# A two-block transformer kernel: the modulation as sums along rows of the transposed weight, and head gains loaded once per partition

## The chip, the core and the metric

The program runs on one core of one Trainium2 chip. The metric is the device time of one execution in microseconds (us); times of before are a median of three runs.

## What is computed

The reference is two transformer blocks over 256 tokens of width 1024, all in fp32: the first with three attention branches, a memory attention and a gated feed-forward layer, the second with a forgetting attention, a retention and an MLP. The second block is modulated: six vectors of 1024 come from one condition vector c, and the outputs of its heads are normalized with a gain of their own.

```
c_act = silu(c)                                        # c: 1 x 1024
mod = einsum('bd,de->be', c_act, w_ada) + b_ada        # w_ada: 1024 x 6144
shift_m, scale_m, gate_m, shift_f, scale_f, gate_f = split(mod, 6)
h = rms(x) * (1 + scale_m) + shift_m
...
fq = rms(fq) * q_norm_gain;  fk = rms(fk) * k_norm_gain            # gains of 64, the same for 8 heads
fox = (rms(fox) * fox_out_gain) * sigmoid(f_og)
ret = (rms(ret) * ret_out_gain) * silu(r_gate)
x = x + gate_m * (concat(fox, ret) @ w_out)
h = rms(x) * (1 + scale_f) + shift_f
x = x + gate_f * (square(relu(h @ w_mlp_in)) @ w_mlp_out)
```

## The kernel before

Tokens stand in two tiles of 128 partitions. Every weight comes as tiles `raw` of 128 x 1024 fp32 (0.5 MB), which ScalarE rounds to `wh` and VectorE (DVE) turns into the rest `wl` (`cols`); each product is then three matmuls (`mm3`). A norm ends in `transpose_split`: TensorE transposes the normed tile `xn` and ScalarE and DVE write it as `aT`, which the next matmuls read. The last products of a stage are done for token tile 0 first and then, behind it, for tile 1 (`out_steps`), so that the norm of tile 0 runs beside the matmuls of tile 1.

The program is written as generators that record operations (`Plan.add`); nothing of it is issued in the order of the code. `Plan.run` goes through a model of time with a price for every operation (`cost`), gives each engine the operation that is due first, and gives tiles their slots in pools of fixed size (`SLOTS`: 12 tiles of 1 KB a partition, 14 of 2 KB, 37 of 4 KB and small ones). What comes out is one fixed order for each engine; each engine works through its own in order, and SyncE issues all transfers in one order. `TUNING` shifts due times by windows of matmuls. All instructions carry line 629, where they are issued, so groups are told apart by the names of their tiles.

The modulation is cut into 12 parts of 512 columns (`modulation`, `mod_part`, started by `next_part` in the merge of the first block, in its feed-forward layer and in the MLP). A part clears `acc` on GpSimd (POOL), loads the bias into its first row, loads `w_ada` with 8 of its rows to a partition, and adds them up on DVE with c as a scalar of each partition, 8 sums of 128 x 512. Then POOL sums over the 128 partitions, and the row goes to DRAM (`mod_rows`). `mod(i)` reads it back as a row broadcast to all partitions, `modrow`:

```
for j0 in range(0, 8, 2):
    nc.sync.dma_start(r, self.mod_w[:, j0:j0 + 2, c0:c0 + 512])
    for j in range(2):
        nc.vector.scalar_tensor_tensor(acc, r[:, j, :], self.mod_c[:, j0 + j:j0 + j + 1], acc, ALU.mult, ALU.add)
nc.gpsimd.partition_all_reduce(acc, acc, channels=P, reduce_op=bass_isa.ReduceOp.add)
```

POOL also does the powers of all norms (`rstd`, `row_rstd`: `s<-s,mhalf`). In `block2_mix`, `rep_row` loads the two gains of 64 repeated 8 times into `qkg`, and the output gains into `og`, which line 1986 scales by 0.5 on DVE: the gates are computed as 1 + tanh of half the argument, which is twice the sigmoid.

Of the kernel before, what the change touches and what calls it, by code (L numbers as in the profile page):

```python
# [16 lines left out]
ALU = mybir.AluOpType  # L17
# [10 lines left out]
EPS = 1e-6  # L28
# [245 lines left out]
class Plan:  # L274
# [146 lines left out]
    @staticmethod  # L421
    def cost(o, views):
        if not views:
            return 1.29
        n = max(math.prod(v.shape[1:]) for v in views)
        psum = any(v.root.kind == "ps" for v in views)
        if o.eng == "pe":
            if o.name == "transpose":
                return 0.11
            n, dt = math.prod(o.args[0].shape[1:]), o.args[1].dtype  # L430
            one = max(0.213, n / 600) if dt == F32 else max(0.104 if dt == F32R else 0.054, n / 2400)
            return one * (0.6 if dt == F32 and o.args[0].shape[0] in (32, 64) else 1.0) + 0.003
        if o.eng == "act":
            return (0.051 if psum else 0.094) + n / 1200 + 0.093 * (isinstance(o.kw.get("scale"), View)
                                                                    + isinstance(o.kw.get("bias"), View) + ("accum_out" in o.kw))
        if o.eng == "dve":
            if o.name == "reciprocal":
                return 0.07 + 0.0062 * n
            fast = not psum and o.name in ("tensor_copy", "tensor_scalar")
            small = o.name in ("tensor_scalar", "scalar_tensor_tensor") and len(views) > (2 if fast else 3)  # L440
            return 0.068 + n / (1920 if fast else 960) + 0.06 * small
        if o.eng == "pool":
            if o.name == "partition_all_reduce":
                return 3.57
# [187 lines left out]
class Net:  # L632
# [133 lines left out]
        yield  # L766


    def rstd(self, ssq, n, width):
        nc = self.nc  # L770
        ms = self.small(n)
        nc.vector.tensor_scalar(ms, ssq, 1.0 / width, EPS, ALU.mult, ALU.add)
        r = self.small(n)
        nc.gpsimd.tensor_tensor(r, ms, self.mhalf[:, :n], ALU.pow)
        return r
# [904 lines left out]


    def modulation(self):
        nc, a = self.nc, self.a
        self.mod_w = a["w_ada_2"].rearrange("(p j) n -> p j n", p=P)
        self.mod_rows = self.tile("dram", DM, nm="mod_rows")[0:6]
        c, s = (self.fixed(8, f"mod_{n}") for n in "cs")
        nc.sync.dma_start(c, a["c_2"].rearrange("a (p j) -> (a p) j", p=P))
        nc.vector.tensor_scalar(s, c, -80.0, None, ALU.max)
        nc.scalar.activation(s, s, AF.Exp, scale=-1.0)
        nc.vector.tensor_scalar(s, s, 1.0, None, ALU.add)  # L1690
        nc.vector.reciprocal(s, s)
        nc.vector.tensor_tensor(s, s, c, ALU.mult)
        self.mod_c = s

    def mod_part(self, q):

        nc = self.nc
        c0 = q * 512
        acc = self.k(2, [P, 512], nm="mod")
        nc.gpsimd.memset(acc, 0.0)  # L1700
        nc.sync.dma_start(acc[0:1, :], self.a["b_ada_2"][:, c0:c0 + 512])
        for j0 in range(0, 8, 2):
            raw = self.k(4, [P, 1024], nm="raw")
            r = raw.rearrange("p (k n) -> p k n", k=2)
            nc.sync.dma_start(r, self.mod_w[:, j0:j0 + 2, c0:c0 + 512])
            yield
            for j in range(2):
                nc.vector.scalar_tensor_tensor(acc, r[:, j, :], self.mod_c[:, j0 + j:j0 + j + 1], acc, ALU.mult, ALU.add)
        yield
        nc.gpsimd.partition_all_reduce(acc, acc, channels=P, reduce_op=bass_isa.ReduceOp.add)  # L1710
        if q // 2 in (1, 4):
            yield
            nc.vector.tensor_scalar(acc, acc, 1.0, None, ALU.add)
        yield
        nc.sync.dma_start(self.mod_rows[q // 2:q // 2 + 1, c0 % DM:c0 % DM + 512], acc[0:1, :])

    def next_part(self):
        if not self.mod_parts:
# [41 lines left out]
    def block2_mix(self, x, u, done):  # L1760
        nc, a, flow = self.nc, self.a, self.flow
# [14 lines left out]
        raw = self.k(4, [P, DM], nm="onehot")  # L1776
# [1 line left out]
        nc.sync.dma_start(raw[:40], a["const_b"][:40, slice(*AT_B["onehot"])])  # L1778
        nc.scalar.activation(onehot.rearrange("p a b -> p (a b)"), raw, AF.Copy)

        def rep_row(src, n, rep, off, tl):
            nc.sync.dma_start(tl[:, off:off + n * rep].rearrange("p (a b) -> p a b", a=rep),
                              bass.AP(tensor=src.tensor, offset=src.offset, ap=[[0, P], [0, rep], [1, n]]))

        qkg = self.k(4, [P, DM], nm="qkg")
        rep_row(a["q_norm_gain_2"], 64, 8, 0, qkg)
        rep_row(a["k_norm_gain_2"], 64, 8, 512, qkg)
        og = self.k(4, [P, DM], nm="og")
        rep_row(a["fox_out_gain_2"], 512, 1, 0, og)
        rep_row(a["ret_out_gain_2"], 512, 1, 512, og)  # L1790
        bf = self.small(8)
        src = a["b_forget_2"]
        nc.sync.dma_start(bf, bass.AP(tensor=src.tensor, offset=src.offset, ap=[[0, P], [1, 8]]))
# [3 lines left out]
        spl = [None, None]  # L1797
        v, rv = ([h[:, 0, :] for h in self.two(nm, (1, 512))] for nm in ("fv", "rv"))

        def head_rstd(src, nh, d):  # L1800
            sq = self.k(2, [P, nh, d], nm="sq")
            nc.scalar.activation(sq, src, AF.Square)
            yield
            ss = self.small(nh)
            nc.vector.tensor_reduce(ss, sq, AX, ALU.add)
            r = self.rstd(ss, nh, d)
            yield
            return r
# [347 lines left out]
```

## Time and profile before

| | |
|---|---|
| time, median of 3 runs | 787.75 us (786.53 to 788.32) |
| the profiled execution: time, span | 789.33 us, 787.5 us |
| TensorE (PE) busy | 750.9 us, 95% |
| DVE busy | 601.9 us, 76% |
| ACT (ScalarE), POOL busy | 393.2 us, 95.2 us |
| mean granted TensorE clock | 0.979 |
| HBM read | 159.68 MB, mean 204 GB/s |

The page's share of busy time tells which engine is full; the time that can be saved lies where PE is not. PEld is the loading of weights into TensorE beside PE. "issue" in a bracket is time in which an engine waited for nothing that the profile shows.

### The profile page before, as it was taken

How to read it: one execution, taken by the hardware profiler on the slowest of the kernel's cores; microseconds unless marked ns; L12 is line 12 of the kernel's file. 1: busy time of each engine (PE TensorE's matmuls, PEld its weight loads, DVE VectorE, ACT ScalarE, POOL GpSimd, SP SyncE). 2: the span in 40 equal slices, each digit the busy share in tenths (PEclk: the TensorE clock that was granted, in tenths of full speed). 3: DMA queues.
4: the chain of work that ended last, by engine and by line, in shares of the span. 5: the costliest groups of instructions: out<-in, count | busy, mean ns of one | idle time of the engine just before them, and what ended most of it. 6: DMA issues, size and time to landing. Idle time of an engine off the chain costs nothing.

```text
span 787.5 us, 13291 instructions
## 1 busy us (share of the span) xinstructions
PE 750.9 (95%) x5195; PEld 684.6 (87%) x5195; DVE 601.9 (76%) x937; ACT 393.2 (50%) x650; POOL 95.2 (12%) x74
## 2 busy tenths in 40 slices
PE   6999999979998999999999389999999999999998
PEld 3989899979897999999998268898887999999996
DVE  4999999979799996978463388889759897755522
ACT  5685684336378434344252165564646644554510
POOL 0111002222000220222200022011101022000000
PEclk9999999989999999999999769999999999999999
DMA  9819566937584597999783538445436885654501
GB/s 313 288 61 271 165 227 218 349 152 264 180 277 150 181 330 265 293 297 312 253 263 80 187 90 198 104 142 172 167 113 249 286 288 212 220 193 166 178 1 54
DMA packets 93811, 161.63 MB, mean 205 GB/s; under 512 B 8019, under 2 KB 44019, under 8 KB 93748
## 3 DMA queue, kind: packets, MB, share of 16 engines
q1 hardware_dynamic: 93748, 160.78, 61.7%
q8 instruction: 41, 0.67, 0.3%
q14 instruction: 22, 0.18, 0.1%
HBM read 159.68 MB, written 1.07 MB: 204 GB/s over the span
## 4 chain that ended last, share of the span: by engine, by line
PE 68%; DVE 6%; DMA 4%; issue 2%; POOL 1%; ACT 0%; SPq 0%; POOLq 0%; DVEq 0%
PE ps L629 68%; DMA og<-in_fox_out_gain_dram 3%; DVE wl L629 1%; DVE x L629 1%; DMA raw<-in_w_in_dram 1%; DVE xn L629 1%; DVE mod L629 1%; DVE s L629 0%; POOL s L629 0%; DVE mk L629 0%; DVE mg L629 0%; DVE mgt L629 0%; DVE prob L629 0%; DVE mq L629 0%; DVE gt L629 0%
## 5 line engine op out<-in xcount | busy, mean ns | idle before, releaser
L629 DVE TENSOR_TENSOR wl<-raw,wh 128x1024 fp32r<-128x1024 f32 (+4 forms) x237 | 292.3, 1259 | 42.9 <-ACT wh L629 27.7
L629 PE MATMUL ps<-aT,wh 128*128 128x256 f32 x1664 | 308.3, 285 | 0.0
L629 ACT ACTIVATE wh<-raw 128x1024 fp32r<-128x1024 f32 (+5 forms) x237 | 240.9, 1042 | 129.4 <-DMA raw<-in_w_ffn_in_dram 30.0
L629 PEld LDWEIGHTS ps<-aT,wh 128*128 128x128 f32 x1664 | 259.2, 189 | 0.7 <-issue 0.4
L629 PE MATMUL ps<-aT,wl 128*128 128x256 f32 x832 | 236.5, 284 | 0.0
L629 PE MATMUL ps<-wh,aT 128*128 128x512 f32 (+5 forms) x672 | 184.6, 360 | 1.2 <-ACT aT L629 0.7
L629 PEld LDWEIGHTS ps<-aT,wl 128*128 128x128 f32 x832 | 157.3, 189 | 0.8 <-issue 0.8
L629 PE MATMUL ps<-wh,hT 128*128 128x512 f32 (+1 forms) x540 | 140.4, 349 | 0.0
L629 PEld LDWEIGHTS ps<-wh,aT 128*128 128x128 f32 x672 | 119.7, 192 | 18.7 <-ACT aT L629 1.3
L629 PE MATMUL ps<-wl,aT 128*128 128x512 f32 (+5 forms) x336 | 118.2, 356 | 0.0
L629 PEld LDWEIGHTS ps<-wh,hT 128*128 128x128 f32 x540 | 94.0, 188 | 14.2
L629 PE MATMUL ps<-wl,hT 128*128 128x512 f32 (+1 forms) x270 | 94.2, 349 | 0.0
L629 DVE SCALAR_TENSOR_TENSOR mod<-raw,mod_s,mod 128x512 f32<-128x512 f32 x96 | 75.3, 786 | 2.3 <-DMA raw<-in_w_ada_dram 1.0
L629 POOL PARTITION_ALL_REDUCE mod<-mod x12 | 49.8, 4148 | 220.2 <-DVE mod L629 212.0
L629 PEld LDWEIGHTS ps<-wl,aT 128*128 128x128 f32 x336 | 64.0, 191 | 8.0 <-DVE wl L629 0.3
L629 PEld LDWEIGHTS ps<-wl,hT 128*128 128x128 f32 x270 | 50.8, 188 | 7.1
L629 POOL TENSOR_TENSOR s<-s,mhalf 128x1 f32<-128x1 f32 (+3 forms) x22 | 24.3, 1108 | 211.6 <-DVE s L629 171.9
L629 PE MATMUL ps<-ident,xn 128*128 128x128 f32 x96 | 23.6, 354 | 26.7 <-DVE xn L629 26.6
L629 PEld LDWEIGHTS ps<-ident,xn 128*128 128x128 f32 x96 | 14.5, 175 | 33.4 <-issue 20.0
L629 ACT ACTIVATE junk<-x 128x512 f32<-128x512 f32 (+1 forms) x29 | 16.0, 554 | 51.2 <-DVE x L629 49.5
L629 DVE TENSOR_TENSOR relu<-relu 128x512 f32<-128x512 f32 x16 | 10.9, 692 | 23.8 <-ACT relu L629 23.7
L629 ACT ACTIVATE aT<-ps 128x256 fp32r<-128x256 f32 (+1 forms) x41 | 17.9, 459 | 21.7 <-PE ps L629 21.4
(280 smaller groups left out, 656.4 us busy)
## 6 DMA issues: line engine op xcount, KB each, us to landing
raw<-in_w_in_dram SPq DMA_DIRECT2D x62, 512.0 KB
raw<-in_w_ada_dram SPq DMA_DIRECT2D x48, 512.0 KB
raw<-in_w_ffn_in_dram SPq DMA_DIRECT2D x44, 512.0 KB
raw<-in_w_mlp_in_dram SPq DMA_DIRECT2D x32, 512.0 KB
raw<-in_w_mlp_out_dram SPq DMA_DIRECT2D x32, 512.0 KB
raw<-in_w_ffn_out_dram SPq DMA_DIRECT2D x22, 512.0 KB
raw<-in_w_out_dram SPq DMA_DIRECT2D x16, 512.0 KB
raw<-in_w_up_dram SPq DMA_DIRECT2D x6, 512.0 KB
```

What stands on the lines that cost most here:

```text
L629: getattr(get[o.eng], name)(*map(real, args), **{k: real(v) for k, v in kw.items()})
```

## The change

The weight of the modulation is given to the kernel transposed (6144 rows of 1024): a layout of the input, made on the host. Of vector i, partition p then holds the 8 outputs p*8 to p*8+7, one row of 1024 each. c is stored to DRAM and read back as a row broadcast to all partitions; each row is multiplied with it on DVE and summed along the row by the same instruction (`accum_out`), 48 sums of 128 x 1024 in all. The results, 8 columns for each vector, get the bias (and 1.0 for the two scales) in one small operation and go to `mod_rows` as 128 pieces of 32 B; the bias is loaded once, as 128 x 6 x 8. The parts run where they ran, two for each vector.

The head gains are loaded once for each partition and broadcast over the 8 heads in the operand of the product. The output gains are not scaled: the 0.5 goes into the power, by multiplying mean square and epsilon with 4 (`part=0.5`). The planner's price of partition_all_reduce is dropped. The planner then orders the whole program anew.

```diff
-    def rstd(self, ssq, n, width):
+    def rstd(self, ssq, n, width, part=1.0):
...
-        nc.vector.tensor_scalar(ms, ssq, 1.0 / width, EPS, ALU.mult, ALU.add)
+        nc.vector.tensor_scalar(ms, ssq, part ** -2 / width, EPS * part ** -2, ALU.mult, ALU.add)
...
     def modulation(self):
...
-        self.mod_w = a["w_ada_2"].rearrange("(p j) n -> p j n", p=P)
-        self.mod_rows = self.tile("dram", DM, nm="mod_rows")[0:6]
-        c, s = (self.fixed(8, f"mod_{n}") for n in "cs")
+        self.mod_w = a["w_ada_2"].rearrange("(i p j) k -> i p j k", i=6, p=P)
+        self.mod_rows = self.tile("dram", DM, nm="mod_rows")[0:7]
+        self.mod_b, self.mod_s = self.fixed(48, "mod_b"), self.fixed(48, "mod_s")
+        nc.sync.dma_start(self.mod_b.rearrange("p (i j) -> p i j", i=6),
+                          a["b_ada_2"].rearrange("a (i p j) -> (a p) i j", i=6, p=P))
+        c, s = (self.small(8, f"mod_{n}") for n in "cs")
...
-        self.mod_c = s
+        nc.sync.dma_start(self.mod_rows[6:7, :].rearrange("a (p j) -> (a p) j", p=P), s)
+        self.mod_c = self.k(4, [P, DM], nm="mod_c")
+        nc.sync.dma_start(self.mod_c, self.mod_rows[6:7, :].to_broadcast([P, DM]))
...
     def mod_part(self, q):
...
+        i = q // 2
+        for j in range(q % 2 * 4, q % 2 * 4 + 4):
+            raw = self.k(4, [P, DM], nm="raw")
+            nc.sync.dma_start(raw, self.mod_w[i, :, j, :])
+            yield
+            nc.vector.scalar_tensor_tensor(raw, raw, 1.0, self.mod_c, ALU.mult, ALU.mult,
+                                           accum_out=self.mod_s[:, i * 8 + j:i * 8 + j + 1])
         yield
-        nc.gpsimd.partition_all_reduce(acc, acc, channels=P, reduce_op=bass_isa.ReduceOp.add)
...
+        if q % 2:
+            s, b = (m[:, i * 8:i * 8 + 8] for m in (self.mod_s, self.mod_b))
+            nc.vector.scalar_tensor_tensor(s, s, 1.0 if i in (1, 4) else 0.0, b, ALU.add, ALU.add)
+            yield
+            nc.sync.dma_start(self.mod_rows[i:i + 1, :].rearrange("a (p j) -> (a p) j", p=P), s)
...
-        qkg = self.k(4, [P, DM], nm="qkg")
-        rep_row(a["q_norm_gain_2"], 64, 8, 0, qkg)
-        rep_row(a["k_norm_gain_2"], 64, 8, 512, qkg)
+        qkg = self.k(1, [P, 2 * 64], nm="qkg")
+        rows(a["q_norm_gain_2"], 64, 0, qkg)
+        rows(a["k_norm_gain_2"], 64, 64, qkg)
...
-                gain = qkg[:, which * 512:(which + 1) * 512].rearrange("p (a b) -> p a b", b=64)
+                gain = qkg[:, None, which * 64:(which + 1) * 64].to_broadcast([P, 8, 64])
...
-            r = yield from head_rstd(mv, nh, d)
+            r = yield from head_rstd(mv, nh, d, 0.5)
...
-        nc.vector.tensor_scalar(og, og, 0.5, None, ALU.mult)
...
+    return {"w_ada_2": np.ascontiguousarray(given["w_ada_2"][0].T)}
```

How the order moves, at three places. The numbers behind the names are those of single tiles.

First, DVE where the second block's norm begins (`block2_norm`; x_68 is the stream, ps the sums of the feed-forward layer). Before:

```order
L629 TENSOR_TENSOR hT_5166<-silu_5091,hT_5166 128x512
L629 TENSOR_TENSOR wl_5176<-raw_5057,wh_5155 128x1024
L629 TENSOR_SCALAR og_5138<-og_5138 128x1024
L629 TENSOR_TENSOR x_68<-ps_3535,x_68 128x512
L629 TENSOR_TENSOR x_68<-ps_3542,x_68 128x512
L629 TENSOR_TENSOR x_68<-x_68,gain_4852 128x512 x2
```

Now:

```order
L627 TENSOR_TENSOR hT_5088<-silu_5021,hT_5088 128x512
L627 TENSOR_TENSOR wl_5098<-raw_4984,wh_5077 128x1024
L627 TENSOR_TENSOR x_68<-ps_3502,x_68 128x512
L627 TENSOR_TENSOR x_68<-ps_3509,x_68 128x512
L627 TENSOR_TENSOR x_68<-x_68,gain_4781 128x512 x2
```

The scaling of og between the last weight and the residual sums is gone; the rest stands as it stood.

Second, POOL around the norm of the memory (the two powers of a 128x1 tile, `s<-s,mhalf`). The ISA rows with names are the reductions over partitions; those without stand wherever POOL goes from them to its other operations and back. Before:

```order
L629 MEMSET mod_1152 128x512
L629 MEMSET mod_1173 128x512
L629 MEMSET mod_1182 128x512
L629 MEMSET mod_1629 128x512
L629 ISA
L629 ISA mod_1152<-mod_1152 128x512
L629 ISA mod_1173<-mod_1173 128x512
L629 ISA mod_1182<-mod_1182 128x512
L629 ISA
L629 TENSOR_TENSOR s_2181<-s_2181,mhalf_70 128x1
L629 TENSOR_TENSOR s_2184<-s_2184,mhalf_70 128x1
L629 ISA
```

Now:

```order
L627 COPY cn_845<-qcn_993 128x64
L627 COPY cn_845<-qcn_1000 128x64
L627 TENSOR_TENSOR s_2197<-s_2197,mhalf_70 128x1
L627 TENSOR_TENSOR s_2200<-s_2200,mhalf_70 128x1
L627 TENSOR_TENSOR s_2625<-s_2625,mhalf_70 128x1
```

Nothing stands between the copies of the sparse attention and the powers, and the next norm's power follows at once.

Third, DVE between the memory attention (`prob` its weights, moT its output) and the residual sums of x. Before:

```order
L629 TENSOR_SCALAR prob_3007<-prob_3007,s_3047 128x256 x4
L629 COPY mv_3070<-ps_2921 128x256
L629 TENSOR_TENSOR wl_3074<-raw_2758,wh_2880 128x1024
L629 TENSOR_TENSOR wl_3092<-raw_2768,wh_2893 128x1024
L629 TENSOR_TENSOR moT_3105<-ps_3081,moT_3105 128x2x128
L629 TENSOR_TENSOR wl_3110<-raw_2822,wh_2913 128x1024
L629 TENSOR_TENSOR moT_3105<-ps_3096,moT_3105 128x2x128
L629 TENSOR_TENSOR wl_3125<-raw_2942,wh_3043 128x1024
L629 TENSOR_TENSOR x_68<-ps_3114,x_68 128x512
```

Now:

```order
L627 TENSOR_SCALAR prob_2953<-prob_2953,s_3007 128x256 x2
L627 TENSOR_TENSOR wl_3054<-raw_2796,wh_2908 128x1024
L627 TENSOR_TENSOR wl_3060<-raw_2942,wh_3011 128x1024
L627 TENSOR_TENSOR wl_3074<-raw_2948,wh_3022 128x1024
L627 TENSOR_TENSOR wl_3087<-raw_2958,wh_3042 128x1024
L627 TENSOR_TENSOR wl_3091<-raw_2967,wh_3058 128x1024
L627 TENSOR_TENSOR moT_3093<-ps_3078,moT_3093 128x2x128
L627 SCALAR_TENSOR_TENSOR raw_3062,mod_s_1657<-raw_3062,mod_c_1470 128x1024
L627 TENSOR_TENSOR moT_3093<-ps_3045,moT_3093 128x2x128
L627 SCALAR_TENSOR_TENSOR raw_3068,mod_s_1657<-raw_3068,mod_c_1470 128x1024
L627 TENSOR_TENSOR x_68<-ps_3097,x_68 128x512
```

Five splits of a weight and two sums of the modulation stand there in place of four splits.

## Rows read from the trace of the kernel before

**Rows 1.** The page, its parts 1 and 2: busy time, share of the span and number of instructions of each engine; and, in 40 equal slices of the span (19.7 us each), the busy share of DVE and the granted TensorE clock, in tenths.

```profile
PE 750.9 (95%) x5195; PEld 684.6 (87%) x5195; DVE 601.9 (76%) x937; ACT 393.2 (50%) x650; POOL 95.2 (12%) x74
...
DVE  4999999979799996978463388889759897755522
...
PEclk9999999989999999999999769999999999999999
```

**Rows 2.** [...]

```profile
160.00:180.00 20.00, 15.68 (x110) 14.66 (x109) 14.12 (x21) 8.99 (x12) 6.05 (x4) 0.83 0.38 142
...
200.00:220.00 20.00, 20.00 (x130) 18.06 (x129) 15.54 (x26) 8.02 (x18) 2.55 (x3) 1.00 0.64 203
...
220.00:240.00 20.00, 19.70 (x176) 18.47 (x174) 19.14 (x40) 15.88 (x37) 0.00 (x0) 1.00 0.83 276
...
240.00:260.00 20.00, 17.23 (x111) 15.71 (x111) 17.80 (x34) 14.29 (x29) 1.74 (x3) 0.91 0.36 119
...
440.00:460.00 20.00, 4.80 (x12) 2.48 (x12) 13.30 (x29) 9.48 (x26) 4.12 (x5) 0.61 0.55 188
```

**Rows 3.** PE in order of time around us 440: start, duration, operation, and in brackets the idle time before it and what ended it.

```profile
430.33 0.39 PE L629 MATMUL ps<-wl,hT 128*128 128x512 f32 x1
...
438.84 0.28 PE L629 MATMUL ps<-wl,hT 128*128 128x256 f32 x1
...
452.69 1.27 PE L629 MATMUL ps<-ident,xn 128*128 128x128 f32 x4 [13.58 <-DVE xn L629]
```

**Rows 4.** DVE in order of time, same stretch, same columns.

```profile
446.11 0.69 DVE L629 TENSOR_SCALAR og<-og 128x1024 f32<-128x1024 f32 x1 [20.06 <-DMA og<-in_ret_out_gain_dram]
...
446.71 1.28 DVE L629 TENSOR_TENSOR x<-ps,x 128x512 f32<-128x512 f32 x2
...
456.16 0.98 DVE L629 TENSOR_SCALAR x<-x,s 128x1024 f32<-128x1024 f32 x1
```

**Rows 5.** The DMA queue of SyncE in order of time: when a transfer is issued and how long the issue takes.

```profile
419.45 0.38 SPq L629 DMA_DIRECT2D qkg<-in_q_norm_gain_dram  x1
...
420.50 5.02 SPq L629 DMA_DIRECT2D og<-in_fox_out_gain_dram  x1
```

**Rows 6.** Stretches of 4 us around us 440, columns as in rows 2.

```profile
420.00:424.00 4.00, 4.00 (x29) 3.68 (x28) 1.51 (x2) 1.30 (x2) 0.00 (x0) 1.00 0.10 31
...
452.00:456.00 4.00, 1.68 (x6) 1.13 (x7) 3.94 (x8) 2.87 (x8) 1.44 (x3) 0.50 0.18 66
...
456.00:460.00 4.00, 3.12 (x8) 1.35 (x6) 3.96 (x11) 3.74 (x11) 1.97 (x3) 0.50 0.52 119
...
460.00:464.00 4.00, 4.00 (x14) 3.25 (x14) 3.56 (x10) 2.61 (x6) 0.00 (x0) 0.50 0.25 79
...
464.00:468.00 4.00, 4.00 (x17) 3.19 (x16) 3.39 (x3) 2.79 (x4) 0.00 (x0) 0.89 0.45 94
```

**Rows 7.** PE in order of time around us 170.

```profile
172.05 0.47 PE L629 MATMUL ps<-ident,xn 128*128 128x128 f32 x1 [3.64 <-DVE xn L629]
```

**Rows 8.** Stretches of 4 us behind it, columns as in rows 2.

```profile
172.00:176.00 4.00, 3.27 (x12) 2.46 (x13) 4.00 (x7) 0.00 (x0) 0.00 (x0) 0.50 0.02 5
176.00:180.00 4.00, 4.00 (x28) 4.00 (x27) 3.96 (x7) 2.83 (x5) 1.64 (x1) 0.73 0.77 271
```

**Rows 9.** POOL in order of time, us 120 to 185.

```profile
159.16 4.14 POOL L629 PARTITION_ALL_REDUCE mod<-mod  x1 [17.30 <-DVE mod L629]
170.62 1.12 POOL L629 TENSOR_TENSOR s<-s,mhalf 128x1 f32<-128x1 f32 x2 [7.32 <-issue]
```

**Rows 10.** DVE in order of time, us 148 to 182.

```profile
160.37 3.27 DVE L629 SCALAR_TENSOR_TENSOR mod<-raw,mod_s,mod 128x512 f32<-128x512 f32 x2
...
171.24 2.74 DVE L629 SCALAR_TENSOR_TENSOR xn<-mx,s,gain 128x512 f32<-128x512 f32 x4 [5.81 <-POOL s L629]
```

**Rows 11.** PE at the norm ahead of the last MLP, in order of time.

```profile
602.19 1.23 PE L629 MATMUL ps<-ident,xn 128*128 128x128 f32 x6 [0.99 <-DVE xn L629]
```

**Rows 12.** Stretches behind the norms at us 250 and 600, columns as in rows 2.

```profile
250.00:252.00 2.00, 2.00 (x11) 2.00 (x11) 2.00 (x6) 1.01 (x3) 0.00 (x0) 0.50 0.00 0
...
252.00:254.00 2.00, 2.00 (x14) 2.00 (x14) 1.49 (x5) 1.98 (x4) 0.00 (x0) 0.68 0.00 0
...
600.00:610.00 10.00, 8.90 (x42) 6.50 (x42) 9.56 (x19) 8.39 (x15) 0.82 (x2) 1.00 0.97 368
```

**Rows 13.** Instructions of the tile mod (sums of the modulation): number, min/median/max ns, first and last start, forms.

```profile
L629 DVE SCALAR_TENSOR_TENSOR mod<-raw,mod_s,mod x96: 732/747/2732, 112.0 to 654.9; 128x512 f32<-128x512 f32 x96
```

**Rows 14.** The same for the tile wl (low parts of the weights).

```profile
L629 DVE TENSOR_TENSOR wl<-raw,wh x237: 622/1219/3266, 11.9 to 748.6; 128x1024 fp32r<-128x1024 f32 x111, 128x452 fp32r<-128x452 f32 x2, 128x768 fp32r<-128x768 f32 x2, 128x904 fp32r<-128x904 f32 x1
```

**Rows 15.** Groups of instructions, shapes apart: number, busy us, mean ns, idle time before them.

```profile
L629 DVE TENSOR_TENSOR aT<-ps,aT 128x512 fp32r<-128x512 f32 x15 | 9.9, 685 | 0.6 <-ACT aT L629 0.6
...
L629 ACT ACTIVATION_READ_ACCUMULATOR junk<-x 128x1 f32 x29 | 5.4, 186 | 0.0
```

**Rows 16.** Stretch of 1 us in the first loads, columns as in rows 2.

```profile
20.00:21.00 1.00, 1.00 (x7) 0.92 (x6) 1.00 (x2) 1.00 (x3) 0.00 (x0) 1.00 1.07 393
```

**Rows 17.** ACT in order of time, us 0 to 70: the first split of a weight that was issued after the loads of the modulation.

```profile
31.40 1.06 ACT L629 ACTIVATE wh<-raw 128x1024 fp32r<-128x1024 f32 x1
```

**Rows 18.** The DMA queue of SyncE in order of time, us 66 to 160, columns as in rows 5.

```profile
99.59 3.15 SPq L629 DMA_DIRECT2D raw<-in_w_up_dram  x2
...
110.50 1.71 SPq L629 DMA_DIRECT2D raw<-in_w_ada_dram  x2
```

More of the change, by code (lines that the diff above doesn't have):

```diff
@@ L442, in cost @@
         if o.eng == "pool":
-            if o.name == "partition_all_reduce":
-                return 3.57
             if o.name == "memset":
@@ L1692, in modulation @@
         nc.vector.tensor_tensor(s, s, c, ALU.mult)
-        self.mod_c = s
+        nc.sync.dma_start(self.mod_rows[6:7, :].rearrange("a (p j) -> (a p) j", p=P), s)
+        self.mod_c = self.k(4, [P, DM], nm="mod_c")
+        nc.sync.dma_start(self.mod_c, self.mod_rows[6:7, :].to_broadcast([P, DM]))
     def mod_part(self, q):
         nc = self.nc
[L1698 to L1705, printed above, removed]
+        i = q // 2
+        for j in range(q % 2 * 4, q % 2 * 4 + 4):
+            raw = self.k(4, [P, DM], nm="raw")
+            nc.sync.dma_start(raw, self.mod_w[i, :, j, :])
             yield
-            for j in range(2):
-                nc.vector.scalar_tensor_tensor(acc, r[:, j, :], self.mod_c[:, j0 + j:j0 + j + 1], acc, ALU.mult, ALU.add)
+            nc.vector.scalar_tensor_tensor(raw, raw, 1.0, self.mod_c, ALU.mult, ALU.mult,
+                                           accum_out=self.mod_s[:, i * 8 + j:i * 8 + j + 1])
         yield
-        nc.gpsimd.partition_all_reduce(acc, acc, channels=P, reduce_op=bass_isa.ReduceOp.add)
-        if q // 2 in (1, 4):
+        if q % 2:
+            s, b = (m[:, i * 8:i * 8 + 8] for m in (self.mod_s, self.mod_b))
+            nc.vector.scalar_tensor_tensor(s, s, 1.0 if i in (1, 4) else 0.0, b, ALU.add, ALU.add)
             yield
-            nc.vector.tensor_scalar(acc, acc, 1.0, None, ALU.add)
-        yield
-        nc.sync.dma_start(self.mod_rows[q // 2:q // 2 + 1, c0 % DM:c0 % DM + 512], acc[0:1, :])
+            nc.sync.dma_start(self.mod_rows[i:i + 1, :].rearrange("a (p j) -> (a p) j", p=P), s)
     def next_part(self):
@@ L1779, in block2_mix, with rows @@
         nc.scalar.activation(onehot.rearrange("p a b -> p (a b)"), raw, AF.Copy)
-        def rep_row(src, n, rep, off, tl):
-            nc.sync.dma_start(tl[:, off:off + n * rep].rearrange("p (a b) -> p a b", a=rep),
-                              bass.AP(tensor=src.tensor, offset=src.offset, ap=[[0, P], [0, rep], [1, n]]))
-        qkg = self.k(4, [P, DM], nm="qkg")
-        rep_row(a["q_norm_gain_2"], 64, 8, 0, qkg)
-        rep_row(a["k_norm_gain_2"], 64, 8, 512, qkg)
+        def rows(src, n, off, tl):
+            nc.sync.dma_start(tl[:, off:off + n], bass.AP(tensor=src.tensor, offset=src.offset, ap=[[0, P], [1, n]]))
+        qkg = self.k(1, [P, 2 * 64], nm="qkg")
+        rows(a["q_norm_gain_2"], 64, 0, qkg)
+        rows(a["k_norm_gain_2"], 64, 64, qkg)
         og = self.k(4, [P, DM], nm="og")
-        rep_row(a["fox_out_gain_2"], 512, 1, 0, og)
-        rep_row(a["ret_out_gain_2"], 512, 1, 512, og)
+        rows(a["fox_out_gain_2"], 512, 0, og)
+        rows(a["ret_out_gain_2"], 512, 512, og)
         bf = self.small(8)
@@ L1798, in block2_mix, with head_rstd @@
         v, rv = ([h[:, 0, :] for h in self.two(nm, (1, 512))] for nm in ("fv", "rv"))
-        def head_rstd(src, nh, d):
+        def head_rstd(src, nh, d, part=1.0):
             sq = self.k(2, [P, nh, d], nm="sq")
@@ L1805, in head_rstd @@
             nc.vector.tensor_reduce(ss, sq, AX, ALU.add)
-            r = self.rstd(ss, nh, d)
+            r = self.rstd(ss, nh, d, part)
             yield
@@ L2131, in views @@
     for k, ap in aps.items():
-        if k in ("b_ada_2", "c_2", "norm_final", "const_a", "const_b"):
+        if k in ("b_ada_2", "c_2", "w_ada_2", "norm_final", "const_a", "const_b"):
             out[k] = ap
@@ L2136, in views, with EXTRA @@
     return out
+def EXTRA(given):
+    return {"w_ada_2": np.ascontiguousarray(given["w_ada_2"][0].T)}
 def kernel(**inputs):
@@ L2146 @@
     given["const_a"], given["const_b"] = CONST_A, CONST_B
+    given.update(EXTRA(given))
     for name, arr in given.items():
```

## The prediction

> **What bounds the kernel now.** I read the page first: TensorE is busy for 750.9 of 787.5 us, DVE for 601.9 [rows 1]. So time can only come out of the 36.6 us in which PE idles, and out of the slices in which its clock is not granted. The clock line has one dip, where the second block's normalization begins [rows 1]. The table of stretches then shows where PE idles: 15.20 us in us 440 to 460, 4.32 in 160 to 180, 2.77 in 240 to 260 [rows 2]; most of the rest is the first loads and the last store. I call these places A (440), B (170) and C (250). Each is a norm that every following matmul needs.
>
> At **A** the list of PE shows the last matmul at 438.84 and the first transposition at 452.69, 13.58 us later, released by DVE [rows 3]. The list of DVE says why: its queue stood 20.06 us at the scaling of og by 0.5, which waited for og's load; the residual sum x<-ps, the head of the norm, is the very next instruction [rows 4]. And og came late because the gains qkg were issued ahead of it [rows 5], each row copied 8 times to each of 128 partitions, 2048 pieces of 256 B: behind their issue the queue moved 31 GB/s [rows 6], against 393 where whole weights stream [rows 16]. At **B** PE ran out at 168.41 and waited 3.64 us [rows 7]. DVE waited 5.81 us for a power on POOL [rows 10], and POOL had ended a partition_all_reduce at 163.30 and then stood 7.32 us with no releaser at all [rows 9]. In its order an ISA row without operands stands at just that place, between the reductions and the powers.
>
> **The change, part by part.** *Scaling of og removed, gains loaded once per partition (A).* Both the waiting instruction and 1792 of the 2048 pieces go. The order of DVE shows x<-ps directly behind a wl that needs only its weight. PE idles 15.20 us in us 440 to 460 [rows 2] and 0.88 before that, from 439.12 [rows 3]: 16.08. What stays? The last matmul of the first token tile is at 430.33, 8.5 us before that of the second [rows 3], and its norm needed 6 us from x<-ps to the first transposition, 446.71 to 452.69 [rows 3, 4], so it is hidden. The second tile's is not. The nearest row is the same hand-over ahead of the last MLP, which cost PE 0.99 us [rows 11]; this norm has two more operations in DVE's queue, x<-x,s of 0.98 us [rows 4] and the product of 256 columns with the final gain, some 0.4 by the price of a column below. I take 2.4 us; bounds 1.0 and 5. Gain 13.7. The clock is the second part: after the idle time it was at its lower level. Busy time of 1.68+3.12+4.00 us at 0.50 and 4.00 at 0.89 [rows 6] is a loss of 4.4+0.44 = 4.8 us. With 0.99 us idle the clock stayed at 1.00, with 2.77 it fell, and cost 2.00x0.50+2.00x0.32 = 1.6 [rows 2, 11, 12]; between them I charge 0.8. Gain 4.0. A: 17.7 us (bounds 13 and 20).
>
> *Sums along rows in place of partition_all_reduce (B).* All 12 reductions, their code changes and the 12 memsets leave POOL; the two powers are the next thing in its queue. Then DVE sets when the memory's norm begins. Up to there it now has 16 sums of 1024 columns where it had 28 of 512, and one wl less. A sum of 512 has a median of 0.747 us [rows 13]; 512 further columns cost 1.219-0.685 = 0.534 [rows 14, 15], so 1.28 without the written accumulator. No row of DVE shows that one; bounds are nothing and the 0.186 us of ScalarE's [rows 15]. I take the middle, 1.37. 16x1.37 - 28x0.747 - 1.22 = -0.2 us: no change. But DVE lost time beside the reductions: 3.27 us for two sums in place of 1.49 while one ran [rows 9, 10], single ones of 2.73 for a sum and 3.27 for a wl [rows 13, 14], together 5.8. DVE was ready at 165.43 (171.24 less 5.81 [rows 10]), so the norm could begin at 159.4 to 165.2; two powers and a first xn, 1.12+0.69 = 1.8 us [rows 9, 10], end at 167.0 at the latest, before PE runs out at 168.41. The idle 4.32 us [rows 2] shrink to some 0.3, and the clock's loss, 3.27x0.50+4.00x0.27 = 2.7 us [rows 8], goes. B: 6.7 us (bounds 3 and 7). [...]
>
> *DVE's work elsewhere.* 48x1.37 = 66 us in place of 96x0.747 = 72: off the path, nothing. The planner gives C another order: between the residual sums of the mixer and those of the memory attention stand three wl and two sums more, 3x1.22+2x1.37 = 6.4 us, against 5.3 us that DVE idles in 200 to 240 [rows 2]. I charge C 1.0 us; bounds a loss of 4 and, if its idle time and clock all went, a gain of 2.77+1.64 = 4.4.
>
> *New transfers.* The bias now comes early, as 768 pieces of 32 B. At the 8.3 ns a piece that 31 GB/s make of 256 B [rows 6] this is a hole of 6.4 us in the queue. What covers it: that queue runs ahead. The first weight behind it lands at about us 22 (an estimate: by the loads' sizes 6.9 MB stand before it, at up to 393 GB/s [rows 16]) and is read at 31.40 [rows 17]. Nothing, then; without that cover up to 6.4. The vector c goes to DRAM and back as a broadcast row, and the queue is held until the store has landed. Held is what comes next, w_up's loads and more of w_ada; there the queue stood anyway from 102.74 to 110.50 [rows 18], and DVE's first sum comes behind both masks of the compressed scores. Nothing; bound 3.
>
> Sum: -17.7-6.7+1.0 = **-23.4**. The profiled execution took 789.33 us (its span is 787.5), so 765.9; the median of the runs shown is 1.6 below it: **764 us**.
>
> **Rivals.** *The accumulating sum runs at half rate.* For: no row shows this form. Against: the sum without it reads two fp32 tensors from SBUF as well and takes hardly more than other sums of 512 columns, 0.747 us against 0.685 [rows 13, 15]. At 1.043 ns a column (0.534 us for 512) it would cost 2x1.07 + 0.2 + 0.1 = 2.44 us, 1.07 more. At B 16x1.07 = 17 us push the first xn from 161.2 to 178.3: PE idles 9.9 us instead of 3.64 and the clock falls as before, +6.3. In the ffn 22 such sums take 17.8 us more than the 48 they replace, and DVE's six slices there, at 9, 9, 6, 9, 7 and 8 tenths [rows 1], have about 20 us to spare: +3. In all -17.7+6.3+3+1 = -7.4: 780 us. [...]
>
> *Slower: the accumulating sum is far dearer.* One mechanism, the same place. At the longest DVE time of 1024 columns in the trace, 3.27 us [rows 14], each costs 1.90 more: B's norm is ready 30 us later, PE idles 23.2 there (+19.6), the ffn's 36 us overrun its 20 by 16, C pays 3.8: -17.7+19.6+16+3.8+1 = +22.7, 810 us. It decides from about 2.7 us a sum.
>
> *Late weights eat half of A.* PE comes to the second block 14 us earlier, and the weights of fk are issued only as slots come free behind the same norm. For: the queue's weights stand behind the decay tables and og. Against: the four weights of fq are issued ahead of og and need no wait, and each later one takes 1.3 us of the queue (0.5 MB at 393 GB/s [rows 16]). Half of A: 773 us.
>
> *A does not close*, because another wait stands behind og's and the change does not do what it says. Against: x<-ps follows og's scaling by 0.6 us, its matmuls had ended 16 us before. B and C alone: 782 us.
>
> **Chances.** Forecast 0.71 (756 to 773 by its bounds), late weights 0.11, half rate 0.08, A stays 0.04, far dearer 0.04, no change 0.02. The range 756 to 779 takes in the first two and leaves out the rest. A measurement tells 0.2%, 1.6 us, from no change: faster 0.94, same 0.02, slower 0.04.
>
> **What would show it.** Right: no DVE wait for og; PE's longest idle time at A under 3 us and the clock near 1.00 in that slice; POOL without ISA rows between the powers and no idle time of PE at 168; sums of 1.3 to 1.5 us. Wrong: sums over 2 us; a wait of ACT for raw behind A; PE idling over 5 us at C; or DVE standing at x<-x,gain, which would mean the final gain is late.

## The result and the profile after

The changed kernel takes **765.1 us** (median of 4 runs, 764.52 to 766.21), the kernel before 787.14 (784.74 to 788.32): a ratio of 0.9725, 95% interval 0.9698 to 0.9753. Forecast: 764, range 756 to 779. The profiled execution took 764.62 us, with a span of 762.8; by its own terms the forecast for it was 765.9.

The page after, engine rows, then slices of 19.1 us (against [rows 1]):

```profile
PE 745.2 (98%) x5195; PEld 680.7 (89%) x5195; DVE 572.8 (75%) x936; ACT 396.5 (52%) x653; POOL 37.3 (5%) x49
...
DVE  6999999899699975787454788888579886555512
...
PEclk9999999999999999999999999999999999999999
```

PE idles 17.6 us of its span where it idled 36.6, the dip in the clock line is gone, and POOL's busy time fell from 95 to 37 us. Stretches of 20 us, against [rows 2]: start and end, length, then busy us and number of instructions of PE, PEld, DVE, ACT and POOL, the granted clock as a share of full speed, the DMA share and GB/s; what was at 440 is now at 420:

```profile
0.00:20.00 20.00, 15.40 (x53) 10.58 (x54) 12.72 (x25) 13.71 (x24) 1.70 (x8) 1.00 0.90 314
160.00:180.00 20.00, 20.00 (x173) 20.00 (x173) 18.37 (x21) 12.67 (x17) 0.00 (x0) 1.00 0.79 270
220.00:240.00 20.00, 16.49 (x114) 13.33 (x113) 19.57 (x37) 12.87 (x33) 0.00 (x0) 0.91 0.75 253
240.00:260.00 20.00, 17.47 (x142) 16.43 (x141) 18.46 (x33) 13.51 (x24) 1.41 (x4) 1.00 0.53 160
420.00:440.00 20.00, 18.08 (x95) 14.88 (x94) 15.96 (x35) 11.63 (x31) 4.12 (x5) 0.91 0.48 157
440.00:460.00 20.00, 20.00 (x91) 16.22 (x90) 17.88 (x23) 11.10 (x14) 4.51 (x2) 1.00 0.81 159
```

A and B closed, and C got worse: 6.0 us idle in its two stretches, where there were 3.1 in 220 to 260 before. The first 20 us, on which the prediction has no term, gained 3.2 us (12.24 us busy before).

**A.** DVE in order of time, against [rows 4]:

```profile
423.03 1.38 DVE L627 TENSOR_TENSOR x<-ps,x 128x512 f32<-128x512 f32 x2 [4.04 <-PE ps L627]
...
427.88 0.69 DVE L627 TENSOR_TENSOR x<-ps,x 128x512 f32<-128x512 f32 x1 [0.33 <-PE ps L627]
...
432.36 0.41 DVE L627 TENSOR_TENSOR x<-ps,x 128x256 f32<-128x256 f32 x1
```

and the waits of PE there, against [rows 3]:

```profile
433.64 0.49 PE L627 MATMUL ps<-wh,aT 128*128 128x512 f32 x1 [0.68 <-ACT aT L627]
434.72 0.50 PE L627 MATMUL ps<-wh,aT 128*128 128x512 f32 x1 [0.59 <-DVE aT L627]
436.10 0.79 PE L627 MATMUL ps<-wh,aT 128*128 128x512 f32 x1 [0.64 <-ACT wh L627]
```

The residual sum now waits only for the matmul that makes it, and in place of one wait of 13.58 us stand three of 0.6 to 0.7.

**B.** POOL (against [rows 9]) and DVE (against [rows 10]):

```profile
158.66 1.06 POOL L627 TENSOR_TENSOR s<-s,mhalf 128x1 f32<-128x1 f32 x2 [83.80 <-DVE s L627]
```

```profile
157.23 1.22 DVE L627 TENSOR_TENSOR wl<-raw,wh 128x1024 fp32r<-128x1024 f32 x1
158.37 0.33 DVE L627 TENSOR_SCALAR s<-s 128x1 f32<-128x1 f32 x2
...
159.24 2.74 DVE L627 SCALAR_TENSOR_TENSOR xn<-mx,s,gain 128x512 f32<-128x512 f32 x4 [0.47 <-POOL s L627]
```

DVE waits 0.47 us for the power where it waited 5.81, and the first xn is ready at 160 us; in the kernel before PE ran out at 168.41 [rows 7].

**The sums**, number, min/median/max ns (against [rows 13]):

```profile
L627 DVE SCALAR_TENSOR_TENSOR raw<-raw,mod_c x48: 1211/1219/1227, 113.8 to 627.0; 128x1024 f32<-128x1024 f32 x48
L627 DVE DVE_READ_ACCUMULATOR raw<-raw,mod_c x48: 78/82/84, 114.9 to 628.1; 128x1 f32 x48
```

1.30 us a sum with its accumulator; the prediction took 1.37.

**C.** PE's waits (total, times, longest), in the kernel before in 220 to 256 us, now in 220 to 243, and DVE in order of time:

```profile
PE ps L629 <- DVE xn L629: 2.6, 2, 2.2
PE ps L629 <- DVE prob L629: 0.2, 1, 0.2
```

```profile
PE ps L627 <- DVE prob L627: 2.1, 1, 2.1
PE ps L627 <- DVE xn L627: 1.6, 1, 1.6
PE ps L627 <- ACT moT L627: 0.5, 1, 0.5
PE ps L627 <- ACT pT L627: 0.5, 1, 0.5
PE ps L627 <- DVE moT L627: 0.3, 1, 0.3
```

```profile
220.88 2.48 DVE L627 TENSOR_REDUCE s<-ps 128x2 f32<-128x512 f32 x4
223.40 2.36 DVE L627 TENSOR_TENSOR wl<-raw,wh 128x1024 fp32r<-128x1024 f32 x2
...
226.08 1.67 DVE L627 TENSOR_SCALAR prob<-prob,s 128x256 f32<-128x256 f32 x6
...
228.79 5.76 DVE L627 TENSOR_TENSOR wl<-raw,wh 128x1024 fp32r<-128x1024 f32 x5
234.47 0.41 DVE L627 TENSOR_TENSOR moT<-ps,moT 128x256 fp32r<-128x256 f32 x1
```

Two weight splits stand between the softmax's maxima and its products, and five more ahead of moT. PE waits 2.1 us for prob and 0.3 for DVE's moT; the wait for xn was there before too.

### The profile page after: what moved, and what is told of

Its sections match the earlier page's. It is cut to its first block, busy times and chain, and to the rows that moved or that the text cites. A ratio compares the mean times of both kernels' runs of the same rounds, so it can differ in the third digit from the quotient of the medians.

```text
span 762.8 us, 13170 instructions
## 1 busy us (share of the span) xinstructions
PE 745.2 (98%) x5195; PEld 680.7 (89%) x5195; DVE 572.8 (75%) x936; ACT 396.5 (52%) x653; POOL 37.3 (5%) x49
## 4 chain that ended last, share of the span: by engine, by line
PE 92%; DVE 6%; issue 1%; ACT 0%; POOL 0%; DMA 0%; POOLq 0%; SPq 0%; DVEq 0%; ACTq 0%
PE ps L627 92%; DVE wl L627 2%; DVE xn L627 1%; DVE x L627 1%; DVE s L627 0%; DVE qa L627 0%; DMA row<-in_norm_mix_dram 0%; DVE prob L627 0%; DVE gt L627 0%; DVE qi L627 0%; ACT aT L627 0%; DVE aT L627 0%; DVE ka L627 0%; POOL s L627 0%; POOL xn L627 0%
## 5 line engine op out<-in xcount | busy, mean ns | idle before, releaser
L627 DVE TENSOR_TENSOR wl<-raw,wh 128x1024 fp32r<-128x1024 f32 (+4 forms) x237 | 278.0, 1201 | 59.5 <-ACT wh L627 37.6
L627 PE MATMUL ps<-wh,aT 128*128 128x512 f32 (+5 forms) x672 | 182.0, 356 | 2.1 <-ACT aT L627 0.7
L627 DVE SCALAR_TENSOR_TENSOR raw<-raw,mod_c 128x1024 f32<-128x1024 f32 x48 | 57.2, 1220 | 4.7 <-DMA raw<-in_w_ada_dram 4.4
L627 ACT ACTIVATE junk<-x 128x512 f32<-128x512 f32 (+1 forms) x29 | 16.1, 555 | 38.1 <-DVE x L627 36.4
L627 ACT ACTIVATE relu<-ps 128x512 f32<-128x512 f32 x16 | 9.6, 599 | 30.0 <-PE ps L627 29.2
L627 ACT ACTIVATE prob<-ps,s 128x256 f32<-128x256 f32 (+1 forms) x48 | 20.1, 452 | 6.4 <-DVE s L627 6.4
L627 PE MATMUL ps<-ident,xn 128*128 128x128 f32 x96 | 19.0, 313 | 3.9 <-DVE xn L627 3.9
L627 DVE TENSOR_TENSOR aT<-ps,aT 128x256 fp32r<-128x256 f32 (+1 forms) x41 | 20.0, 515 | 3.6 <-ACT aT L627 3.6
```

The costliest lines, as they stand in the source:

```text
L627: getattr(get[o.eng], name)(*map(real, args), **{k: real(v) for k, v in kw.items()})
```

## The experiments

All kernels in one table: the median time, and PE's losses at each place from the profiled execution, as idle time + time lost to the clock (summed over stretches of 4 us: 4 less PE's busy time; busy time times 1 less the granted clock). In the kernel before one matmul of 512 columns starts 0.43 us behind the other at a granted clock of 0.50 (463.19 to 463.62) and 0.23 at 1.00 (469.54 to 469.77). The places are the first 20 us; 160 to 200 (B); 200 to 280 (C); 416 to 500 (A). Elsewhere the losses are 5.0 to 5.4 us in every kernel, and PE's busy time times clock is 740 to 744 us in all of them, so that this table holds the difference between two kernels to within 4 us. Its first row is the execution that the prediction rests on. The kernel before was run beside each: its median was 787.1 to 787.3 us there, and 786.0 beside e8, e9 and e10; the ratios are to those.

| kernel | us | start | B | C | A |
|---|---|---|---|---|---|
| before, first profile | 789.3 (this run) | 7.8 | 4.3+2.8 | 3.1+1.6 | 16.1+4.8 |
| before, second (e9) | 786.0 | 6.6 | 3.9+2.7 | 3.1+1.6 | 15.0+3.8 |
| **the change** | **765.1** | 4.6 | 0 | 6.1+1.5 | 1.9+1.7 |
| e1 gains once | 770.9 | 6.5 | 4.5+1.5 | 2.9+1.5 | 2.1+1.5 |
| e2 no scaling | 779.2 | 6.7 | 4.3+2.9 | 3.0+1.6 | 7.4+3.8 |
| e3 both of these | 771.1 | 6.4 | 4.0+2.3 | 3.1+1.6 | 2.1+1.6 |
| e8 no scaling, 1152 pieces | 771.6 | 6.7 | 4.0+2.7 | 3.1+1.6 | 2.5+1.7 |
| e4 modulation alone | 784.6 | 4.6 | 0 | 7.2+3.2 | 16.2+3.9 |
| e10 e4, ffn's wl later | 778.5 | 4.9 | 0 | 2.6+1.5 | 17.8+4.4 |
| e5 the change, ffn's wl later | 759.0 | 4.8 | 0 | 2.2+1.7 | 2.0+1.5 |
| e6 the change, sums twice | 774.9 | 4.9 | 7.3+1.6 | 6.1+1.4 | 2.0+0 |
| e7 the change, one reduction | 768.0 | 6.6 | 0 | 7.0+3.1 | 1.9+1.6 |

### A: which of the two edits

**e1**, the kernel before with

```diff
-        qkg = self.k(4, [P, DM], nm="qkg")
-        rep_row(a["q_norm_gain_2"], 64, 8, 0, qkg)
-        rep_row(a["k_norm_gain_2"], 64, 8, 512, qkg)
+        qkg = self.k(1, [P, 2 * 64], nm="qkg")
+        rows(a["q_norm_gain_2"], 64, 0, qkg)
+        rows(a["k_norm_gain_2"], 64, 64, qkg)
```

> The kernel before, with one part of the change: the gains of q and k are loaded once per partition and repeated by the access pattern when they are used; og is still scaled by 0.5, and the modulation is the old one. Theory (the scaling waits only because 2048 small pieces stand ahead of og): og lands some 15 us earlier, DVE does not stand at the scaling, PE's idle time at the second block's norm falls from 16 us to 2 to 3, and the whole gain of place A is had by this edit alone: 17 us, 770 us. Rival (the scaling itself holds DVE, since og is issued behind the weights anyway): DVE still waits over 8 us for og and the time stays above 778 us.

770.87 us, ratio 0.9789 (0.9771 to 0.9806). DVE at the scaling of og:

```profile
423.33 0.69 DVE L629 TENSOR_SCALAR og<-og 128x1024 f32<-128x1024 f32 x1 [0.63 <-DMA og<-in_ret_out_gain_dram]
```

The scaling is still there and waits 0.63 us in place of 20.06. The theory holds, but the edit moves the loads as well: their tile is smaller and comes from another pool, and in the new order the 256 pieces that are left are issued at 371.2 and 372.7 us, no longer just ahead of og (419.45 in the kernel before); in e3 and in the change (374.1) it is the same. Fewer pieces and an earlier issue are told apart only by e8.

**e2**, the kernel before with

```diff
-            r = yield from head_rstd(mv, nh, d)
+            r = yield from head_rstd(mv, nh, d, 0.5)
...
-        nc.vector.tensor_scalar(og, og, 0.5, None, ALU.mult)
```

> The kernel before, with the other part of the change at place A: og is not scaled (its factor goes into the root mean square), while the gains are still loaded as 2048 pieces of 256 B. Theory (either edit is enough for A): nothing in DVE's queue ahead of the norm waits for og, PE's idle time there falls to 2 to 3 us, and the time is 770 us. Rival (late weights: the small pieces still hold up the queue, and PE, 14 us earlier, meets them at fk's weights or at the gains): PE or ACT waits for a transfer in the 30 us behind the norm, half of the gain goes, 778 us.

779.16 us, ratio 0.9895 (0.9874 to 0.9915): the rival's number. ScalarE, and PE behind it:

```profile
444.01 1.06 ACT L629 ACTIVATE onehot<-onehot 128x1024 fp32r<-128x1024 f32 x1 [6.28 <-DMA onehot<-in_const_b_dram]
```

```profile
446.19 0.80 PE L629 MATMUL ps<-wh,aT 128*128 128x512 f32 x1 [6.77 <-ACT aT L629]
```

With the first waiter gone, the next transfer behind the pieces is late: onehot, a table whose first matmul is at 498 us, but whose cast stands in ScalarE's queue ahead of the copies aT. It isn't a weight, as the rival had it; the way it works is the rival's. My theory that either edit is enough was wrong.

**e3**, both edits and the old modulation.

> The kernel before with both edits of place A and the old modulation. Theory: the term of A alone, 17 us: 770 us; PE's idle time of 3.6 us near 170 us stays, and POOL stands some 9 us ahead of its first work at the start, as before. Rival (the two edits do separate things): more gain than the larger of the two kernels with one edit each, by over 2 us.

771.14 us, ratio 0.9787 (0.9765 to 0.9808), the same as e1. Without the pieces the scaling costs nothing.

**e8**, e2 with the gain of q loaded once (`rep_row(..., 64, 1, 0, qkg)`, broadcast in the product) and that of k still 8 times.

> The kernel before without the scaling of og, and with the gain of q loaded once per partition while that of k is still repeated 8 times: 1152 pieces of 256 B in place of 2048. Without the scaling and with all pieces the time was 779.2 us: ScalarE, which holds the copies of the norm's transpositions, stood 6.3 us at the table onehot, whose load came behind the pieces at 444.0 us. Theory (each piece holds the queue some 8.3 ns): 896 pieces fewer bring onehot 7.4 us earlier, to 436.6 us, just before ScalarE asks for it at 437.7; its wait goes and the time is that with no small pieces at all, 771 us (to 773). Rival (the hold-up is the switch to such loads or to the repeated reading, not their number): onehot still lands after 441 us and the time stays above 776 us.

771.56 us, ratio 0.9817 (0.9803 to 0.9832). The same row of ScalarE:

```profile
438.22 1.06 ACT L629 ACTIVATE onehot<-onehot 128x1024 fp32r<-128x1024 f32 x1 [1.00 <-DMA onehot<-in_const_b_dram]
```

Counted from the issue of the gains (418.87 us in e2, 418.35 here), onehot landed after 25.1 and 19.9 us: 5.3 us for 896 pieces, 5.9 ns each, less than the 8.3 that I had taken. That is what the next load gained, not what a piece takes: by the packets of the trace the 2048 pieces start between 419.9 and 443.0 us in e2 and the 1152 between 419.3 and 433.7 here, 11 and 13 ns each. From 421 to 431 us the queue moved 14 to 23 GB/s in both, with a DMA share of 0.05 to 0.09, about one of the 16 engines; the 31 GB/s of [rows 6] take in the end of another load. The gains are issued where they were in e2, so the number of pieces is the cause at A. Why such pieces are slow, their size or the repeated reading of one row, is not shown.

### The modulation, and place C

**e4**, the kernel before with the new `modulation` and `mod_part` alone.

> The kernel before with the new modulation alone (sums along rows, no partition_all_reduce); scaling and gains are the old ones. By the traces of before and after: place B closes (7 us of idle time and clock), the start is 3 us shorter, place C loses 3 us: 780 us, and PE still idles 15 us at the second block's norm. By the terms of the prediction alone (B 6.7, C +1.0): 781 us. Rival (the start of 0 to 20 us differs between executions by chance, not by the program): POOL's first work begins at 9.5 us as in the kernel before, PE idles 7.8 us in the first 20 us, and the time is 783 us.

784.55 us, ratio 0.9959 (0.9943 to 0.9975): less of a gain than any of the three numbers. B and the start did what the theory says; C lost 10.3 us where it lost 4.6 before. DVE's order there is that of the changed kernel, which lost 7.5. The difference is where the clock fell. Stretches of 4 us, of e4 and then of the change:

```profile
226.00:230.00 4.00, 3.08 (x31) 2.50 (x32) 4.00 (x13) 4.00 (x6) 0.00 (x0) 1.00 0.94 336
...
234.00:238.00 4.00, 2.96 (x9) 2.41 (x10) 3.60 (x7) 0.00 (x0) 0.00 (x0) 0.71 0.35 122
238.00:242.00 4.00, 3.96 (x21) 3.25 (x20) 2.44 (x6) 1.91 (x6) 0.07 (x1) 0.87 0.00 0
...
246.00:250.00 4.00, 4.00 (x23) 3.96 (x22) 3.70 (x9) 3.24 (x7) 0.00 (x0) 0.59 0.15 16
```

```profile
226.00:230.00 4.00, 3.42 (x26) 2.86 (x28) 4.00 (x13) 4.00 (x5) 0.00 (x0) 0.73 0.95 329
230.00:234.00 4.00, 2.89 (x27) 1.73 (x24) 4.00 (x5) 1.88 (x5) 0.00 (x0) 0.84 0.97 317
234.00:238.00 4.00, 3.69 (x16) 2.72 (x17) 4.00 (x8) 1.05 (x2) 0.00 (x0) 1.00 0.38 130
```

In the change the low clock (0.50 in 228 to 230 us) fell while PE would next have to wait for DVE's five wl anyway, and it then waited 0.3 us for moT; in e4 it came there at full clock and waited 1.5, and the low clock fell on the output matmuls behind, and once more behind the norm. Why it fell where it did in either is not settled.

**e5**, the changed kernel with one entry more in the planner's table:

```diff
-    (1.5, 8.0, 0.0, 1.0, ((('ffnnorm_0', 'pe'), -2), (('memk', 'act'), 2), (('memnorm_0', 'dve'), -4))),
+    (1.5, 8.0, 0.0, 1.0, ((('ffnnorm_0', 'pe'), -2), (('memk', 'act'), 2), (('memnorm_0', 'dve'), -4), (('ffn', 'dve'), -8))),
```

> The changed kernel with one number more in the planner's table: in the window of dense matmuls that holds the memory attention, the ffn's work on DVE (the wl of its weights) counts as due 8 us later. Nothing is computed otherwise; the order of DVE now has the softmax and moT ahead of seven wl that stood before them. Theory (place C lost about 3 us because these wl stand ahead of prob and moT): PE's wait of 2.1 us for prob goes, its idle time in 200 to 280 us falls from 6.1 to 3 us, 762 us. Rival (the wl only fill time in which DVE would wait, and C is set by the norm's own chain): PE waits as long at xn or at the first wh of the ffn, 765 us; or the ffn's wl come too late and PE waits for them, 767 us.

**758.98 us** (758.46 to 759.74), ratio 0.9642 (0.9623 to 0.9662): better than both kernels, and twice the gain expected. DVE, and PE's waits in 200 to 280 us:

```profile
220.37 2.12 DVE L627 TENSOR_REDUCE s<-ps 128x2 f32<-128x512 f32 x3
...
224.45 1.14 DVE L627 TENSOR_SCALAR prob<-prob,s 128x256 f32<-128x256 f32 x4
225.51 2.35 DVE L627 TENSOR_TENSOR wl<-raw,wh 128x1024 fp32r<-128x1024 f32 x2
227.78 0.42 DVE L627 TENSOR_TENSOR moT<-ps,moT 128x256 fp32r<-128x256 f32 x1
```

```profile
PE ps L627 <- DVE xn L627: 2.2, 1, 2.2
```

The only wait of PE that is left is the norm's own. Between the maxima and the norm stand two wl and two sums less than in the change, 5.0 us of DVE by their rows, so the edit takes work out of the place besides turning its order. From the first transposition at B to the first at C the change took 76.9 us (165.10 to 241.96) and e5 71.2 (164.84 to 236.07): 3.0 us less idle time, 1.6 less of low clock, and 1.0 that the records of PE do not place. Behind C e5 pays the low clock after all (1.7 us, the change 0.1), and takes as long from there as the change, 521.0 and 520.8 us, with 0.9 us less idle time. So at C the table has 3.9 us less idle time and 0.2 more of low clock, of the 5.6 us by which the two profiled executions differ; where the rest of the gain comes from is not shown.

**e10**, e4 with the same entry.

> The kernel before with the new modulation alone and the planner's one number that holds the ffn's wl back; scaling and gains are the old ones. Alone the new modulation gave only 2.6 us, and the two edits at A 16.0 us, together 18.6 where the whole change gave 22. Theory (the missing 3 us are place C: with the new modulation alone its idle time and its clock cost 10.3 us in the profile, with the whole change 7.5): with C's order mended the modulation is worth 2.6+10.3-3.9 = 9 us: 778 us. Rival (the missing part lies at A, where PE arrives earlier and waits for og as long): 781 us or more.

778.49 us, ratio 0.9899 (0.9882 to 0.9916): the time of the theory, but against the kernel before beside it (786.03) a gain of 7.5 us, not 9. C closed as the theory has it; A lost 22.1 us, where e4 has 20.1 and the second profile of before 18.8. DVE at the scaling in e10, and in the second profile of before:

```profile
434.67 0.69 DVE L629 TENSOR_SCALAR og<-og 128x1024 f32<-128x1024 f32 x1 [22.00 <-DMA og<-in_ret_out_gain_dram]
```

```profile
443.82 0.69 DVE L629 TENSOR_SCALAR og<-og 128x1024 f32<-128x1024 f32 x1 [19.04 <-DMA og<-in_ret_out_gain_dram]
```

og came 26.2 us after the issue of the gains (408.44) and 25.6 (418.18); PE ran out 18.5 and 19.7 us after it. So while A stands, some of what is won ahead of it may be handed back there, as the rival had it; the two profiles of before differ by 2.1 us at A themselves, so that isn't shown. Of the 3.4 us by which the parts alone (16.0 for e3, 2.6 for e4) make less than the whole, 22, C has 2.8 by the table (10.3 in e4, 7.5 in the change).

### The start

**e7**, the changed kernel with, in `mlp` behind the last vector of the modulation,

```diff
+                t = self.k(2, [P, 512], nm="unused")
+                nc.gpsimd.partition_all_reduce(t, self.gate[:, :512], channels=P, reduce_op=bass_isa.ReduceOp.add)
```

> The changed kernel with one partition_all_reduce put back, at the very end of POOL's queue (some 600 us into the run, its result unused). Theory (POOL starts late because the program holds this operation at all: in the four kernels with it the first work on POOL began at 8.4 to 9.5 us with no releaser, in the two without it at 4.7 to 5.4 us, when its data had landed): POOL's first work begins at about 8.4 us, PE idles 6.4 us in place of 4.6 in the first 20 us, 767 us. Rival (the start differs for another reason, such as the rows between the reductions or chance): first work at about 5 us, 765 us.

767.97 us (767.02 to 768.48), ratio 0.9755 (0.9734 to 0.9775). POOL's first work behind its constants, in the first profile of before, in the change, and in e7:

```profile
9.52 0.39 POOL L629 TENSOR_TENSOR both<-ident 128x16 f32<-128x16 f32 x2 [9.09 <-issue]
```

```profile
5.41 0.43 POOL L627 TENSOR_TENSOR both<-ident 128x16 f32<-128x16 f32 x2 [4.96 <-DMA ident<-in_const_a_dram]
```

```profile
8.31 0.39 POOL L627 TENSOR_TENSOR both<-ident 128x16 f32<-128x16 f32 x2 [7.88 <-issue]
```

One reduction, run 630 us later, makes POOL stand 7.9 us with no releaser at the start. The first power is behind it, and with it the first xn and PE: 2.0 us of start. (The medians of e7 and the change differ by 2.9 us, the profiled executions by 3.9; the table has 2.6 more at C too, where the clock fell twice, as in e4.) An ISA row without operands stands just ahead of this work in the order of all three programs, the change too, where POOL began when ident had landed. So that row alone does not make the wait, and why it costs only where the program holds a reduction is not shown.

**e9**, the kernel before again.

> The kernel before once more, unchanged, for a second profile. Its runs spread over 4.6 us (784.7 to 789.3), those of the changed kernel over 1.7, and the execution profiled first was at the slow end, with POOL's first work at 9.5 us where the three other kernels with partition_all_reduce showed 8.4. Theory (part of the spread is when POOL becomes ready at the start): its first work at 8.3 to 8.5 us, PE idle 6.4 to 6.7 us in the first 20 us, a time of 786 to 788 us. Rival: the start is as it was and the spread comes from the places B and A.

786.04 us; POOL's first work at 8.31 us, PE idle 6.6 us in the first 20. But A was shorter too, by 2.1 us of idle time and clock: so both the start and A make up the difference of these two executions, and the one that I worked from was slow at both.

### The price of dearer sums

**e6**, the changed kernel with each sum a second time, 62 us more on DVE.

> The changed kernel with each of the 48 sums along rows done twice, one behind the other (the second on the product that the first left, so the modulation's values are not the reference's): 62 us more on DVE. This prices the prediction's rivals, dearer sums. By the prediction's reckoning (DVE's time up to the memory's norm is tight, the ffn has room): the 16 sums ahead of place B come to 21 us more, of which DVE's idle time in 100 to 160 us covers 6 and a few are slack; PE idles 8 to 15 us near 170 us, the ffn costs nothing or up to 3: 777 us (771 to 785). Rival (DVE is 72 per cent busy, so more work on it is hidden): 765 to 767 us.

774.87 us, ratio 0.9847 (0.9823 to 0.9871): 9.8 us more, inside the range given. PE's waits in 158 to 180 us:

```profile
PE ps L627 <- DVE wl L627: 4.6, 2, 3.3
PE ps L627 <- DVE xn L627: 2.4, 1, 2.4
```

Nearly all of it is at B (7.3 us idle, 1.6 of clock), as reckoned, though PE stood first at the wl of the weights and then at xn; the ffn paid nothing. The rival falls: DVE's share is 75% in the change's page, and work added to it was not hidden at B.

## Why the prediction was right, step by step

Against its own execution the forecast was -23.4 us to 765.9; it came to -24.7. By term, from the table (first and third row; sums of idle time and clock):

- **A**: -17.7 forecast, -17.3 measured. 1.9 us idle for 2.4, and 1.7 of clock for 0.8. The cause given was the right one in part: it named the scaling and the pieces as one; e1 and e8 show that the pieces are the cause, and e2 that taking away the scaling alone gives only half of it. That the pieces left would also be issued 45 us earlier, the prediction did not say.
- **B**: -6.7 forecast, -7.1 measured. Nothing is left of it.
- **C**: +1.0 forecast, +2.9 measured. The step that failed is the reckoning of the additions against DVE's idle time in 200 to 240 us. The idle time that came, 3.0 us, is PE's at prob, pT and moT, behind wl that stand ahead of them in DVE's queue, and such waits a sum over 40 us can't show. e5 and e10, with these wl later, have them gone; as less work stands there too, they do not part the order from the amount.
- **The start**: no term; -3.2 measured in this execution, -2.0 against the second profile of before. The prediction followed the reductions to B and not to the head of POOL's queue.
- **DVE elsewhere and the new transfers**: nothing forecast, nothing seen: in 20 to 160 us PE idles 0.4 us, before 0.5. SyncE's queue stood 2.5 us for the store of c, up to 100.48.

So 0.4 too much at A, 0.4 too little at B, 1.9 missed at C and 3.2 at the start: -1.3 in sum, by luck of opposite signs. The offset of 1.6 us to the median did not carry over either; what made the first execution slow (start, A) is what the change took away.

The rivals: *half rate* falls by the 1219 ns for 1024 columns, with the accumulator read by an instruction of its own (82 ns): the plain difference wl of the same size takes the same 1219 ns [rows 14]. *Far dearer* falls with it, and both were priced too high: at 2.60 us a sum (e6) the kernel takes 775 us, where half rate at 2.44 was to give 780. *Late weights* did not come, a wait of 0.64 us for wh apart; in e2 it did, with a table in the weights' place. *A does not close*: it closed.

## What to carry to other kernels

When a load is late, look at what was issued ahead of it on its queue and count the pieces: here 2048 stood ahead of og, for which DVE waited 20.06 us, and taking away that waiter uncovered the next one, ScalarE at onehot, 6.28 us in e2. A rare operation cost time far from where it runs: one partition_all_reduce, 639 us into the run, cost 2.0 us at the start (e7). And when work is repriced for a planner, read the new order at the short chains between matmuls: one number in its table was worth 6 us here, where the whole change gave 22.

## What was not expected of the hardware

- Pieces of 256 B, each row of a gain read 8 times for each of 128 partitions, took 11 to 13 ns apiece, at 14 to 23 GB/s (e2, e8); 896 of them fewer brought the next load 5.3 us sooner.
- POOL's first work began 8.3 to 9.5 us into the run in the seven profiles of programs with partition_all_reduce (12 of them in six, one in e7), and at 4.7 to 5.8 us, when its data had landed, in the five without.
- The same order of work lost 7.5 or 10.3 us at C, with the granted clock falling at different places behind a wait of PE of 2.1 us for prob.
